# Later loads of one channel tile's up weights, and one tile's deferred convolutions two products later, in a decoder layer with a ConvFFN

## The chip, the cores and the metric

The kernel runs on one core of one Trainium2 chip. The metric is the time of one execution in microseconds (us) on the device. Times of before come from three runs; the profile is of one execution.

## The reference

One decoder layer on 16 meta tokens and 1024 tokens of 1024 features: a mixer (differential attention and a gated recurrence, HGRN2), its output projection, and a feed-forward network with a causal convolution of width 3. The part that matters here is the end of the mixer and the feed-forward network:

```python
mix = jnp.concatenate([y_diff, y_hgrn], axis=-1) @ w_out[l]
h = h + rmsnorm(mix, ln_mix_post[l])
a = rmsnorm(h, ln_ffn_pre[l])
y = conv_ffn(a, w_ffn_up[l], ffn_conv_w[l], ffn_conv_b[l], w_ffn_down[l])
h = h + rmsnorm(y, ln_ffn_post[l])

def conv_ffn(a, w_up, conv_w, conv_b, w_down):
    u = a @ w_up                      # 1024 x 5632
    u = <causal convolution of width 3, one filter per channel>(u) + conv_b
    gate, up = jnp.split(u, 2, axis=-1)
    return (jax.nn.gelu(gate, approximate=True) * up) @ w_down
```

## The kernel before, in words

Every large float32 product is made of three passes: each operand is split into a rounded part ("h") and its rest ("l"), and the matmuls h*h, h*l and l*h are summed. A split is a cast on ScalarE (ACT) and a subtraction on VectorE (DVE) or GpSimd (POOL), issued by the helper `split` at L58's recording wrapper.

Three stages touch the change.

*Output projection and row blocks.* The loop over `i` from 1 to 8 takes a block of 128 tokens. TensorE makes the second half of the projection (`py`); `post(i)` normalizes it on ACT and DVE, adds it to the residual stream in `xh`, stores `xh` to DRAM (`hsc`, L1229), and scales it into `a2`. There are two `xh` buffers, so the load of block i + 2 (L1208) waits for the store of block i. `trans(i - 2)` transposes an earlier block (L1249), and ACT copies it into `at2`.

*Operands of the up products.* `at2` is cut in two token parts, p = 0 and 1. For each part the quarters and their sums and differences become seven split operands `t` (a Strassen-like scheme with seven products). This is a long run of DVE instructions, the `t<-at,t` rows.

*Up products.* Channel tiles are counted by `ft` from 0 to 21. Tile 0 is multiplied plainly (`pq`). From ft = 1 on a tile takes seven products `j` per token part, in the banks `pa`, `pb`, `pc`; DVE combines them (`xu`, `u`, `uu`, `ug`). The seven weight operands of a tile come from four loaded quarters (`ra`, 256 KB each, tags 11, 22, 21, 12; five buffers), POOL sums and differences of them (`ws`), and splits (`uh`, `ul`). `prep(q)` makes operand q % 7 of tile q // 7, and with q % 7 == 0 it issues the four loads. During product j of tile ft the code calls `prep` for tile ft + 1. So the third channel tile (ft = 2) is prepared during ft = 1.

Convolutions are deferred: a finished tile part is put in `later`, and `gated` takes it out during the next tile. `gated` is four DVE instructions for a token part (`c<-ug,cwt,c` and `c<-uu,cwt,c`), a gelu on ACT, a product on POOL and a store to `gsc`.

The order on TensorE is the program's. On the other engines a scheduler sets it at build time; `tc.issue_after(x)` keeps an instruction behind x in the queue of x's engine, with no wait of its own. Each engine and SyncE's DMA queue works in order, so an instruction that waits holds what is behind it.

Of the kernel before, what the change touches and what calls it, by code (L numbers as in the profile page):

```python
# [17 lines left out]
P = 128  # L18
# [72 lines left out]
def layer_kernel(ctx: ExitStack, tc: tile.TileContext, x, meta, table, lbl, gpre, gpost, win,  # L91
# [5 lines left out]
    T, SY = nc.tensor, nc.sync  # L97
# [40 lines left out]
    hsc = dp.tile([SEQ, D], F32, tag="hsc", name="hsc")  # L138
# [30 lines left out]
    def rstd_of(dst, ss, n):  # L169
        A.activation(dst, ss, AF.Ln, bias=eps[: dst.shape[0]], scale=1.0 / n)  # L170
        return A.activation(dst, dst, AF.Exp, scale=-0.5)
# [11 lines left out]
    def long_tile(name):  # L183
        return mix_tile("X0", F32, name)
# [621 lines left out]
    raws, parts = {}, [[None, None] for _ in range(3)]  # L806
# [216 lines left out]
    def tok(i):  # L1023
        return (2, 14) if i == 0 else (P, start(i))
# [46 lines left out]
    blocks, loaded = {}, {}  # L1071
# [60 lines left out]
    at2.reverse()  # L1132
    q_cm, qp = pool("p2", 2, "right")

    raws, sums, made, marks = {}, {}, {}, {}

    def load_raw4(ft):
        raws.clear()
        for nm, m, c in (("11", ft, 0), ("22", ft + NF, 1), ("21", ft + NF, 0), ("12", ft, 1)):
            raws[nm] = swp.tile([P, 512], F32, tag="ra", name=f"ra{ft}_{nm}", bufs=5)  # L1140
            with tc.issue_after(loaded[4].ins):
                SY.dma_start(raws[nm], wup[m][:, 512 * c: 512 * (c + 1)])

    def w_sum(nm, a, b, op):
# [4 lines left out]
    def prep(q):  # L1149
        ft, j = divmod(q, 7)  # L1150
        if ft >= NF or q in made:
            return
        if j == 0:
            load_raw4(ft)
            src = raws["11"]
            w_sum("1", raws["21"], raws["22"], ALU.add)
        elif j == 1:
            src = w_sum("2", sums["1"], raws["11"], ALU.subtract)
        elif j == 2:
            src = sums["1"]  # L1160
        elif j == 3:
            src = w_sum("3", raws["11"], raws["21"], ALU.subtract)
        elif j == 4:
            src = raws["12"]
        elif j == 5:
            src = raws["22"]
        else:
            src = w_sum("4", raws["12"], sums["2"], ALU.subtract)
        where = swp if q % 2 else wp
        hi = where.tile([P, 512], F32R, tag="wh", name=f"uh{q}", bufs=4)  # L1170
        lo = where.tile([P, 512], F32R, tag="wl", name=f"ul{q}", bufs=4)
        split(hi, lo, src, G if j % 2 == 0 and j and (ft > 1 or j != 4) else V, marks.get((ft - 1, 0)) if j == 1 else None)
        made[q] = (hi, lo)
# [3 lines left out]
    def prep_plain():  # L1177
        load_raw4(0)
        for j, nm in enumerate(("11", "12", "21", "22")):
            where = swp if j % 2 else wp  # L1180
            hi = where.tile([P, 512], F32R, tag="wh", name=f"uh{nm}", bufs=4)
            lo = where.tile([P, 512], F32R, tag="wl", name=f"ul{nm}", bufs=4)
            split(hi, lo, raws[nm], G, halved[0])
            plain[nm] = (hi, lo)
# [25 lines left out]
    def post(i, py, free=None):  # L1210
        r, t0 = tok(i)
        xh = xhs.pop(i)
        if i % 2:
            a2 = long_tile(f"a2_{i}")[:, :D]
        elif i == 0:
            a2 = xh
        else:
            a2 = bp.tile([P, D], F32, tag="a2", name=f"a2_{i}", bufs=1)
        tmp = qp.tile([P, 512], F32, tag="tmp", name=f"tmp{i}", bufs=1)
        junk = qp.tile([P, 512], F32, tag="junk", name=f"junk{i}", bufs=1)  # L1220
        s1, s2 = ssy[:r, i, 1:2], ssy[:r, i, 2:3]
        A.activation(junk[:r], py[:r], AF.Square, accum_out=s1)
        V.tensor_tensor(tmp[:r], py[:r], gpo[:r], op=ALU.mult)
        A.activation(s1, s1, AF.Ln, bias=ssy[:r, i, 0:1], scale=1.0 / D)
        A.activation(s1, s1, AF.Exp, scale=-0.5)
        V.scalar_tensor_tensor(xh[:r, :512], y0[:r, i], s1, xh[:r, :512], ALU.mult, ALU.add)
        V.scalar_tensor_tensor(xh[:r, 512:], tmp[:r], s1, xh[:r, 512:], ALU.mult, ALU.add)
        if i:
            SY.dma_start(hsc[P * (i - 1): P * i, :], xh)  # L1229
        if i:  # L1230
            A.activation(a2[:r], xh[:r], AF.Square, accum_out=s2)
        else:
            s3 = ssy[:r, i, 3:4]
            for half, s_ in ((0, s2), (1, s3)):
                A.activation(free[:r], xh[:r, 512 * half:512 * half + 512], AF.Square, accum_out=s_)
            V.tensor_tensor(s2, s2, s3, op=ALU.add)
        marks["scale"] = rstd_of(s2, s2, D)
        marks["normed"] = V.scalar_tensor_tensor(a2[:r], xh[:r], s2, gfb[:r], ALU.mult, ALU.mult)
        a2t[i] = a2
# [61 lines left out]
    for i in range(1, NBLK):  # L1301
# [18 lines left out]
        if i == 1:  # L1320
# [11 lines left out]
            for p in (3, 4):  # L1332
                out_last(p)
            continue
        post(i, py)
        if i == 2:
            post(0, ysum[:, :512], ysum[:, 512:])
# [33 lines left out]
    def gated(ft, p, ug, uu):  # L1371
        cg = conv(ft, p, 0, ug)
        A.activation(cg, cg, AF.Gelu_apprx_tanh)
        cu = conv(ft, p, 1, uu)
        marks["mult"] = G.tensor_tensor(cg, cg, cu, op=ALU.mult)
        marks["store"] = SY.dma_start(gsc[P * ft: P * (ft + 1), C0[p]:C0[p] + 2 * WN[p] - 2], cg)
# [109 lines left out]
    def g_in(k, half, nm):  # L1486
        t = dn.tile([P, 2 * WN[0]], F32, tag="gk", name=f"gi{nm}_{k}")[:, :512]
        SY.dma_start(t, g_src(k, half))
        return t

    def w_in(pr, k):
        t = swp.tile([P, 512], F32, tag="ra", name=f"wi{pr}_{k}", bufs=5)
        if pr in (5, 6, 7, 4):
            SY.dma_start(t, tsc[(5, 6, 7, 4).index(pr)][P * k: P * (k + 1)])
        else:
            kk, half = {1: (k, 0), 2: (k + NH, 0), 3: (k + NH, 1)}[pr]
            SY.dma_start(t, wdown[P * kk: P * (kk + 1), 512 * half: 512 * (half + 1)])
        return t

    def operands(pr, k, loaded=None):  # L1500
        ga, gb, gc, gs = (keep[nm][:, k] if keep else None for nm in ("ga", "gb", "gc", "gs"))
        if pr == 1:
            a = loaded[0] if loaded else g_in(k, 0, "1")
        elif pr == 2:
            SY.dma_start(gb, g_src(k + NH, 0))
            a = gb
        elif pr == 5:
            a = gs
        elif pr == 6:
            V.tensor_tensor(gs, gs, ga, op=ALU.add)  # L1510
            a = gs
        elif pr == 3:
            V.tensor_tensor(gb, gs, gb, op=ALU.subtract)
            a = gb
        elif pr == 7:
            V.tensor_tensor(ga, gc, ga, op=ALU.subtract)
            a = ga
        else:
            a = g_in(k + NH, 1, "4")
        b = loaded[1] if loaded else w_in(pr, k)  # L1520
        nm = f"{pr}_{k}"
        gh = dn.tile([P, 512], F32R, tag="gh", name=f"gh{nm}")
        gl = dn.tile([P, 512], F32R, tag="gl", name=f"gl{nm}")
        split(gh, gl, a, V)
        wh = wp.tile([P, 512], F32R, tag="wh", name=f"wh{nm}", bufs=4)
        wl = wp.tile([P, 512], F32R, tag="wl", name=f"wl{nm}", bufs=4)
        split(wh, wl, b, V)
        return gh, gl, wh, wl

    for ft in range(1, NF):  # L1530
        units = [unit(ft, p, ps_b) for p in range(2)]
        for j in range(7):
            if j != 1:
                with tc.issue_after(marks["gain"].ins) if ft == 1 else nullcontext():
                    prep(7 * (ft + 1) + j)
            for u in units:
                next(u)
            if j in (1, 3):
                with tc.issue_after(marks["last"].ins):
                    gated(*later.pop(0))  # L1540
            if j == 1:
                prep(7 * (ft + 1) + j)
            if ft == NF - 2 and j == 5:
                with tc.issue_after(marks["store"].ins):
                    opens = [(g_in(k, 0, "1"), w_in(1, k)) for k in range(LOOK)]
            if ft == NF - 1 and 1 < j < 5:
                with tc.issue_after(marks["x1"].ins), tc.issue_after(marks[ft, 1].ins):
                    ready[j - 2] = operands(1, j - 2, opens[j - 2])
# [190 lines left out]
```

## Time and profile before

| | us |
|---|---|
| median of three runs (1275.89 to 1278.39) | 1275.97 |
| the profiled execution | 1276.64 |
| its span, first to last instruction | 1274.9 |

Of the span TensorE is busy for 1256.4 us, DVE 914.5, ACT 687.2 and POOL 507.8. The granted clock of TensorE is 0.999. The row blocks lie from about 560 to 620 us, the plain products of tile 0 from 617 to 643 us, and the tiles from ft = 1 on behind them, up to 1045 us.

In the rows of the timeline stand start, duration, engine, line, operation, output<-inputs with the buffer numbers left out, and in brackets how long the engine had been idle and what ended that. In the rows of waits: engine, its tile and line, what it waited for, us in total, times, longest.

### The profile page before, as it was taken

The numbers are of one execution on the slowest core, as the hardware profiler recorded it, in microseconds if no ns is written. First come the engines' busy times: TensorE is split into PE (matmuls) and PEld (weight loads), VectorE is DVE, ScalarE is ACT, GpSimd is POOL, SyncE is SP. The second block draws the span as 40 slices with busy tenths as digits, with TensorE's granted clock in tenths as the row PEclk, the third lists the DMA queues.
The fourth block names the chain that finished last, engine by engine and source line by source line (L and its number), as shares of the span: only waits on it lengthen the run. The fifth ranks groups of instructions, "written<-read, shape, count | busy, mean of one in ns | idle before, by whom it ended". The sixth has DMA issues, their size and how long they took to land.

```text
span 1274.9 us, 26032 instructions
## 1 busy us (share of the span) xinstructions
PE 1256.4 (99%) x10154; PEld 1172.8 (92%) x10154; DVE 914.5 (72%) x1489; ACT 687.2 (54%) x1635; POOL 507.8 (40%) x390
## 2 busy tenths in 40 slices
PE   8999999999999999999999999999999999999997
PEld 7999999999999998778899999999999998888886
DVE  7665646565656564557899888898898877797586
ACT  8475466546654754356764544445535445564554
POOL 5231423241323311353067676676776731020121
PEclk9999999999999999999999999999999999999999
DMA  7335555273734633688322221322222238955363
GB/s 260 96 60 131 89 140 96 80 146 93 132 94 79 125 81 119 217 268 276 129 67 68 92 87 64 100 76 75 92 76 84 75 113 262 355 180 173 91 215 124
DMA packets 116561, 165.04 MB, mean 129 GB/s; under 512 B 10115, under 2 KB 57539, under 8 KB 116438
## 3 DMA queue, kind: packets, MB, share of 16 engines
q1 hardware_dynamic: 93206, 151.84, 37.1%
q0 software_dynamic: 23232, 11.54, 7.7%
q8 instruction: 80, 1.31, 0.4%
q14 instruction: 43, 0.35, 0.1%
HBM read 134.24 MB, written 52.17 MB: 146 GB/s over the span
## 4 chain that ended last, share of the span: by engine, by line
PE 48%; DVE 3%; DMA 1%; ACT 1%; issue 1%; POOL 1%; DVEq 0%; SPq 0%; ACTq 0%; POOLq 0%
PE pd L1586 5%; PE pd L1587 5%; PE pd L1585 5%; PE pb L1412 4%; PE pb L1411 4%; PE pb L1413 4%; PE pa L1412 3%; PE pc L1412 3%; PE pa L1411 3%; PE pc L1411 3%; PE pc L1413 3%; PE pa L1413 3%; PE pq L1390 1%; PE pq L1389 1%; PE pq L1391 1%
## 5 line engine op out<-in xcount | busy, mean ns | idle before, releaser
L1412 PE MATMUL pb<-t,uh 128*128 128x258 f32 x504 | 140.9, 280 | 0.3 <-DVE t L58 0.3
L1411 PE MATMUL pb<-t,uh 128*128 128x258 f32 x504 | 140.5, 279 | 0.8 <-DVE u L58 0.8
L1413 PE MATMUL pb<-t,ul 128*128 128x258 f32 x504 | 140.1, 278 | 0.0
L1586 PE MATMUL pd<-wl,gh 128*128 128x512 f32 x308 | 120.3, 391 | 0.9 <-DVE wl L58 0.9
L1587 PE MATMUL pd<-wh,gl 128*128 128x512 f32 x308 | 120.0, 389 | 0.0
L1585 PE MATMUL pd<-wh,gh 128*128 128x512 f32 x308 | 119.9, 389 | 0.0
L58 DVE SCALAR_TENSOR_TENSOR c<-uu,cwt,c 128x514 f32<-128x514 f32 (+1 forms) x88 | 107.0, 1215 | 0.0
L58 DVE SCALAR_TENSOR_TENSOR c<-ug,cwt,c 128x514 f32<-128x514 f32 (+1 forms) x88 | 101.4, 1153 | 0.0
L1411 PEld LDWEIGHTS pb<-t,uh 128*128 128x128 f32 x504 | 94.8, 188 | 1.0 <-DVE u L58 1.0
L1412 PEld LDWEIGHTS pb<-t,uh 128*128 128x128 f32 x504 | 94.8, 188 | 0.5 <-DVE t L58 0.5
L58 ACT ACTIVATE c<-c 128x514 f32<-128x514 f32 (+1 forms) x44 | 27.9, 634 | 124.7 <-DVE c L58 124.7
L1413 PEld LDWEIGHTS pb<-t,ul 128*128 128x128 f32 x504 | 94.8, 188 | 0.0
L1412 PE MATMUL pa<-t,uh 128*128 128x258 f32 (+1 forms) x336 | 93.9, 280 | 0.0
L1412 PE MATMUL pc<-t,uh 128*128 128x258 f32 (+1 forms) x336 | 93.9, 279 | 0.0
L58 POOL TENSOR_TENSOR ws<-ra,ra 128x512 f32<-128x512 f32 x42 | 69.2, 1648 | 61.8 <-DMA ra<-in_wup_dram 31.4
L1411 PE MATMUL pa<-t,uh 128*128 128x258 f32 (+1 forms) x336 | 93.6, 279 | 0.0
L1411 PE MATMUL pc<-t,uh 128*128 128x258 f32 (+1 forms) x336 | 93.6, 278 | 0.0
L1413 PE MATMUL pa<-t,ul 128*128 128x258 f32 (+1 forms) x336 | 93.4, 278 | 0.0
L1413 PE MATMUL pc<-t,ul 128*128 128x258 f32 (+1 forms) x336 | 93.4, 278 | 0.0
L58 POOL TENSOR_TENSOR ul<-ws,uh 128x512 fp32r<-128x512 f32 x42 | 69.1, 1646 | 60.0 <-PE pa L1413 44.2
L58 POOL TENSOR_TENSOR c<-c,c 128x514 f32<-128x514 f32 (+1 forms) x44 | 67.9, 1543 | 52.6 <-ACT c L58 49.2
L58 DVE TENSOR_TENSOR ul<-ra,uh 128x512 fp32r<-128x512 f32 x43 | 41.5, 966 | 46.6 <-POOL ul L58 46.6
(389 smaller groups left out, 4184.0 us busy)
## 6 DMA issues: line engine op xcount, KB each, us to landing
ra<-in_wup_dram SPq DMA_DIRECT2D x88, 256.0 KB, 2.6
mp<-msc SPq DMA_DIRECT2D x23, 512.0 KB, 5.6
tsc<-in_wdown_dram SPq DMA_DIRECT2D x44, 256.0 KB, 4.8
wi<-tsc SPq DMA_DIRECT2D x44, 256.0 KB, 3.1
gi<-gsc SPq DMA_DIRECT2D x33, 256.0 KB, 4.0
wi<-in_wdown_dram SPq DMA_DIRECT2D x33, 256.0 KB, 5.0
gsc<-c SPq DMA_DIRECT2D x22, 257.0 KB, 2.1
tsc<-in_wdown_dram POOLq DMA_DIRECT2D x22, 256.0 KB, 7.0
```

The costliest lines, as they stand in the source:

```text
L58: ins = call(*args, **kw)
L1389: T.matmul(pt, hi[:, s], th[:, k], start=(kh + k == 0), stop=False)
L1390: T.matmul(pt, hi[:, s], tl[:, k], start=False, stop=False)
L1391: T.matmul(pt, lo[:, s], th[:, k], start=False, stop=(kh == 1 and k == 3))
L1411: T.matmul(pt, hi[:, s], th[:, k], start=(first and k == 0), stop=False, skip_group_check=True)
L1412: T.matmul(pt, hi[:, s], tl[:, k], start=False, stop=False, skip_group_check=True)
L1413: T.matmul(pt, lo[:, s], th[:, k], start=False, stop=(k == 3), skip_group_check=True)
L1585: T.matmul(py, gh[:, s], wh, start=(k == 0 and pr not in (3, 7)), stop=False, skip_group_check=True)
L1586: T.matmul(py, gh[:, s], wl, start=False, stop=False, skip_group_check=True)
L1587: T.matmul(py, gl[:, s], wh, start=False, stop=(k == NH - 1), skip_group_check=True)
```

## The change

The loads of ft = 2 stand behind the store of the seventh row block, `stored[7]`, and no longer behind an early load, `loaded[4]`. The two convolutions that are taken from `later` during ft = 1 (those of tile 0) are issued at the products j = 3 and 5, and no longer at j = 1 and 3. All other tiles stay as they are.

```diff
-    raws, sums, made, marks = {}, {}, {}, {}
+    raws, sums, made, marks, stored = {}, {}, {}, {}, {}
...
-            with tc.issue_after(loaded[4].ins):
+            with tc.issue_after((stored[7] if ft == 2 else loaded[4]).ins):
                 SY.dma_start(raws[nm], wup[m][:, 512 * c: 512 * (c + 1)])
...
-            SY.dma_start(hsc[P * (i - 1): P * i, :], xh)
+            stored[i] = SY.dma_start(hsc[P * (i - 1): P * i, :], xh)
...
-            if j in (1, 3):
+            if j in ((3, 5) if ft == 1 else (1, 3)):
                 with tc.issue_after(marks["last"].ins):
                     gated(*later.pop(0))
```

SyncE's queue at the end of the row blocks. `ra_11_7986`, `ra_22_7988`, `ra_21_7990` and `ra_12_7992` are the four quarters of ft = 2, those of 8249 to 8255 belong to ft = 3; `hsc<-xh_7467` is the seventh store and `hsc<-xh_7521` the eighth.

```order
 L1208 DMA xh_7521<-in_x_dram 128x1024
 L1229 DMA hsc<-xh_7467 128x1024
+L1142 DMA ra_11_7986<-in_wup_dram 128x512
+L1142 DMA ra_22_7988<-in_wup_dram 128x512
+L1142 DMA ra_21_7990<-in_wup_dram 128x512
 L1229 DMA hsc<-xh_7521 128x1024
+L1142 DMA ra_12_7992<-in_wup_dram 128x512
 L1142 DMA ra_11_8249<-in_wup_dram 128x512
 L1142 DMA ra_22_8251<-in_wup_dram 128x512
```

Before, the first of the four left behind the loads of ft = 1, the next two behind the loads of the fourth row block, and the last behind the fourth store. On POOL the order of the three sums that read them (`ws`) is unchanged: they stand behind the last `y<-y,gpo` of the row blocks.

DVE's queue during ft = 1. `c_0_0` is the convolution of tile 0, p = 0; `ul_8079` and `ul_8115` (8068 and 8104 now) are operands 1 and 3 of ft = 2; `u_1_0` and `uu_0` are combinations of ft = 1, p = 0, behind product 3.

```order
 L58 TENSOR_TENSOR xu_0_8003<-pb_0_8037,xu_0_8003 128x258
 L58 TENSOR_TENSOR xu_1_8021<-pb_1_8051,xu_1_8021 128x256
-L58 SCALAR_TENSOR_TENSOR c_0_0_8065<-ug_0_7645,cwt,c_0_0_8065 128x514
-L58 SCALAR_TENSOR_TENSOR c_0_0_8070<-uu_0_7646,cwt,c_0_0_8070 128x514
-L58 SCALAR_TENSOR_TENSOR c_0_0_8065<-ug_0_7645,cwt,c_0_0_8065 128x514
-L58 SCALAR_TENSOR_TENSOR c_0_0_8070<-uu_0_7646,cwt,c_0_0_8070 128x514
-L58 TENSOR_TENSOR ul_8079<-ws_8076,uh_8078 128x512
-L58 TENSOR_TENSOR ul_8115<-ws_8112,uh_8114 128x512
+L58 TENSOR_TENSOR ul_8068<-ws_8065,uh_8067 128x512
+L58 TENSOR_TENSOR ul_8104<-ws_8101,uh_8103 128x512
 L58 TENSOR_TENSOR u_1_0_8004<-pb_0_8037,xu_0_8003 128x258
+L58 TENSOR_TENSOR uu_0_8001<-pc_0_8075,u_1_0_8004 128x258
```

The four instructions of `c_0_0` now stand behind `uu` of both token parts, and those of the second part, `c_0_1`, behind the combinations of product 5. From the first weights of ft = 3 on DVE's queue is as before.

ACT's queue in the same place, now. `uh15_8067` is the cast of operand 1 of ft = 2 and reads the second POOL sum; `t1_5` is the last split of the second token part, and `xu_1_1` the first copy of ft = 1, p = 1.

```order
L58 CAST uh15_8067<-ws2_8065 128x512
L58 CAST t1_5_7960<-at2_1_6973 128x1024
L58 COPY xu_1_1_8021<-pa1_1_8023 128x256
L58 CAST uh16_8071<-ws1_7994 128x512
L58 ACTIVATE c0_0_0_8135<-ug0_0_7645,cbt_85,cwt_84 128x514
L58 ACTIVATE c1_0_0_8140<-uu0_0_7646,cbt_85,cwt_84 128x514
```

The cast of operand 1 stood ahead of the split's cast before, too; what moved is the time at which its POOL sum can have its loads.

## The prediction

> **What bounds the kernel now.** I read the page's engine line first, then the list of what TensorE waited for from 560 us to 700 us, where every moved instruction lies, then the busy time by stretch.
>
> ```profile
> PE 1256.4 (99%) x10154; PEld 1172.8 (92%) x10154; DVE 914.5 (72%) x1489; ACT 687.2 (54%) x1635; POOL 507.8 (40%) x390
> ```
> ```profile
> PE pa L1249 <- DVE a L58: 1.2, 2, 0.7
> PE pb L1411 <- DVE u L58: 0.8, 1, 0.8
> PE pb L1412 <- DVE t L58: 0.3, 1, 0.3
> ```
> ```profile
> 600.00:620.00 20.00, 19.34 (x108) 16.40 (x107) 13.56 (x16) 13.75 (x41) 0.39 (x1) 1.00 0.67 206
> 620.00:640.00 20.00, 19.47 (x166) 19.19 (x165) 19.97 (x19) 17.11 (x31) 0.00 (x0) 1.00 0.19 75
> 640.00:660.00 20.00, 18.86 (x159) 18.46 (x158) 20.00 (x24) 14.94 (x24) 13.98 (x6) 1.00 0.13 40
> 660.00:680.00 20.00, 20.00 (x175) 20.00 (x174) 17.48 (x23) 8.94 (x16) 14.14 (x11) 1.00 0.25 81
> ```
>
> TensorE is the bound, and its matmuls are not changed. Only its waits can go. The stretches' columns are length, PE, weight load, DVE, ACT and POOL busy, clock, DMA share and GB/s. PE is idle for 0.66 + 0.53 + 1.14 = 2.33 us in 600 to 660 us, and not at all from 660 us. At four places it stands still, always for the DVE. A wait costs a little more than its idle time: in the last stretch a matmul starts every 20/175 = 0.114 us, but the one before a wait is counted busy for 0.28 us (rows below), so each of the four costs some 0.17 us more. The ceiling of any gain is therefore 2.33 + 4 x 0.17 = 3.0 us, 0.235% of the time. A measurement of this kernel tells about 0.2%, 2.55 us, from no change. There is no such ceiling on a loss: from 620 to 660 us the DVE is busy 39.97 of 40 us, and what is put on it there comes out on PE.
>
> **What leaves: three sums and four loads from 560 to 604 us.** The third tile's loads feed three POOL sums, which ran here:
>
> ```profile
> 594.73 2.26 POOL L58 TENSOR_TENSOR ws<-ra,ra 128x512 f32<-128x512 f32 x1
> 597.07 1.61 POOL L58 TENSOR_TENSOR ws<-ws,ra 128x512 f32<-128x512 f32 x1
> 598.65 1.74 POOL L58 TENSOR_TENSOR ws<-ra,ra 128x512 f32<-128x512 f32 x1
> 659.25 1.29 POOL L58 TENSOR_TENSOR ws<-ra,ra 128x512 f32<-128x512 f32 x1
> ```
> ```profile
> 596.38 1.16 DVE L58 SCALAR_TENSOR_TENSOR xh<-y,ssy,xh 128x512 f32<-128x512 f32 x1
> 597.46 1.77 DVE L58 SCALAR_TENSOR_TENSOR xh<-tmp,ssy,xh 128x512 f32<-128x512 f32 x1
> 617.25 0.75 DVE L58 SCALAR_TENSOR_TENSOR xh<-tmp,ssy,xh 128x512 f32<-128x512 f32 x1
> ```
>
> The same DVE instruction takes 0.75 us where POOL is idle and 1.77 and 1.16 us beside the sums: they kept it 1.02 and 0.41 us, 1.43 us together. That is on a path to PE:
>
> ```profile
> 599.27 1.06 ACT L58 ACTIVATE a<-xh 128x1024 f32<-128x1024 f32 x1 [3.45 <-DVE xh L58]
> 610.28 0.33 PE L1249 MATMUL pa<-ident,a 128*128 128x128 f32 x1 [0.66 <-DVE a L58]
> 621.12 0.44 PE L1249 MATMUL pa<-ident,a 128*128 128x128 f32 x2 [0.53 <-DVE a L58]
> 619.78 1.28 DVE L58 SCALAR_TENSOR_TENSOR a<-xh,ssy,gfb 128x1024 f32<-128x1024 f32 x1 [1.78 <-ACT ssy L58]
> ```
>
> ACT stood 3.45 us for that xh, with the next block's squares queued behind it; so later blocks' DVE work moves up with it. An advance of 1.43 us covers both waits: PE gains 0.66 + 0.53 + 2 x 0.17 = 1.5 us, and the last "a" and all DVE work behind it start about 1.5 us earlier (the head start). Fewer bytes in the store and load chain of the xh tiles may add to it; between nothing and 1.7 us is possible, and I take 1.5, nearest to the 1.43 of the rows.
>
> **What arrives: the same loads and sums behind the seventh store.** SyncE now issues three loads behind this first store, ahead of the second one, and the fourth behind that:
>
> ```profile
> 618.20 7.43 SPq L1229 DMA_DIRECT2D hsc<-xh  x2
> hsc<-xh SPq DMA_DIRECT2D x6, 512.0 KB, 5.2
> ra<-in_wup_dram SPq DMA_DIRECT2D x6, 256.0 KB, 2.6
> ```
>
> The second store does not leave until 7 us later, so three issues ahead of it cost SyncE nothing. The fourth load waits for the third sum, and the fourth tile's loads stand behind it; those left only from 641 us, so there are 10 us of cover. The loads land after the store ahead of them: between 2.6 us (alone) and 5.2 + 2 x 2.6 us behind 618.2 - 1.5 = 616.7, so from 619 to 627 us; I take 623. The first sum then meets the DVE's longest unbroken run:
>
> ```profile
> 625.20 1.23 DVE L58 TENSOR_TENSOR t<-at,t 128x1032 fp32r<-128x1032 f32 x1
> 629.95 9.28 DVE L58 TENSOR_TENSOR t<-at,t 128x1024 fp32r<-128x1024 f32 x8
> 646.56 1.22 DVE L58 TENSOR_TENSOR t<-at,t 128x1024 fp32r<-128x1024 f32 x1
> 647.84 0.38 PE L1412 MATMUL pb<-t,uh 128*128 128x256 f32 x1 [0.35 <-DVE t L58]
> 631.74 0.28 PE L1390 MATMUL pq<-t,uh 128*128 128x256 f32 x1
> 644.58 6.70 POOL L58 TENSOR_TENSOR ul<-ws,uh 128x512 fp32r<-128x512 f32 x1 [44.18 <-PE pa L1413]
> ```
>
> [...] Bounds: nothing, if sums fall beside DVE work that doesn't mind; 2.26 + 1.61 + 1.74 = 5.6 us, if they hold the DVE for their whole rows. I take three turns, 3.06 us, because mixed DVE work from 622 to 629 us resembles the 597 us place. Less the head start the splits come 3.06 - 1.5 = 1.56 us late. PE waits for the split at 646.56 already, so that is 1.56 us on PE against before. (The split for 631.74, ready by 629.95 + 9.28/8 = 631.11, has 0.63 us of room; it takes part of the delay earlier, not twice.)
>
> [...] The 1.77 us row is less than the two one after the other, 0.75 + 1.29 = 2.04 us, so I keep 1.02.
>
> **The convolutions two blocks later.** Four instructions leave the place ahead of u:
>
> ```profile
> 650.70 1.13 DVE L58 SCALAR_TENSOR_TENSOR c<-ug,cwt,c 128x514 f32<-128x514 f32 x1
> 651.75 1.78 DVE L58 SCALAR_TENSOR_TENSOR c<-uu,cwt,c 128x514 f32<-128x514 f32 x1
> 653.45 1.78 DVE L58 SCALAR_TENSOR_TENSOR c<-ug,cwt,c 128x514 f32<-128x514 f32 x1
> 655.16 1.78 DVE L58 SCALAR_TENSOR_TENSOR c<-uu,cwt,c 128x514 f32<-128x514 f32 x1
> 658.07 0.74 DVE L58 TENSOR_TENSOR u<-pb,xu 128x258 f32<-128x258 f32 x2
> 657.47 0.28 PE L1413 MATMUL pa<-t,ul 128*128 128x256 f32 x1
> 658.53 0.39 PE L1411 MATMUL pb<-t,uh 128*128 128x258 f32 x1 [0.79 <-DVE u L58]
> 652.65 0.60 ACT L58 CAST uh<-ws 128x512 fp32r<-128x512 f32 x1
> ```
>
> They hold 656.86 - 650.70 = 6.2 us. Without them u waits for the cast at 652.65 (0.60), two ul and nothing else: some 654.5 us, 4 us ahead of PE. So the 0.79 + 0.17 = 0.95 us go, even if the splits are 3 us late. The convolutions then run from about 655 us, the second set behind two more combinations; their cover is the DVE's idle 2.5 us of 20 in the last stretch. What could be late next is u of the third tile:
>
> ```profile
> 677.39 0.42 DVE L58 TENSOR_TENSOR u<-pb,xu 128x258 f32<-128x258 f32 x1
> 678.20 0.28 PE L1411 MATMUL pb<-t,uh 128*128 128x258 f32 x1
> ```
>
> It was ready at 677.81, 0.39 us before its matmul. If the convolutions pushed it later by more than that, PE would wait there instead. Its DVE queue is the same as before from the third tile's first weights on, and the two and a half idle microseconds lie ahead of it: cost 0, and what exceeds 0.39 us if that cover is gone.
>
> **The sum.** -1.5 (two waits) is used up where PE catches up with late splits; there PE stands at +1.56, then -0.95: **+0.6 us**. Against the profiled execution's 1276.64 us (span 1274.9 and 1.74 around it) that is 1277.2. The median of the runs shown is 1275.97, 0.67 us less, so on it the forecast is **1276.6 us**; own range 1275.2 (two turns, -0.4, and a little) to 1278.0 (sums of 1.29 us each and a smaller head start).
>
> **Rivals.**
>
> *All waits go (faster).* The loads land while the DVE still does mixed work, the sums fall where it waits for ACT or reads PSUM, and the splits keep their head start. Then PE keeps the 1.5 and gains the 0.95: -2.45 us, at most the ceiling of -3.0; say -2.7, 1273.3 us. For it: the DVE paused 1.78 us for ACT at 619.78. Against it: that pause is before the landing I take, and a DVE busy for 39.97 of 40 us has no free place.
>
> *The sums hold the DVE whole, with no head start (slower).* [...] For it: nothing in the run from 620 to 660 us gives. Against it: ACT's 3.45 us wait names xh's DVE instruction, and 1.77 us is less than two instructions end to end (0.75 + 1.29).
>
> *The sums lose the port (slightly slower).* The 6.70 us row is a POOL instruction of 1.29 us that stood 5.4 us beside back-to-back DVE splits, until these:
>
> ```profile
> 650.03 0.76 DVE L58 TENSOR_TENSOR xu<-pb,xu 128x258 f32<-128x258 f32 x2
> 652.00 0.28 PE L1411 MATMUL pb<-t,uh 128*128 128x258 f32 x1
> ```
>
> So the sums might not run until the DVE itself stops. ACT's order then has the cast of the second sum ahead of the last split's cast and of the second xu copy, and the DVE stops for that cast behind the split at 646.56 and one ul, at 648.4. Two sums (2.6), two casts (0.6 and about 1.0), a split (1.22), an ul and an xu (about 1.1) end at 654.9, where PE wanted xu at 652.00: 2.9 us, less the 0.95: +1.9 us, 1277.9, and with the head start +0.4. It costs less than a delay of every split.
>
> *The edit does nothing.* It could be that the loads would leave no later than before. SyncE's order excludes it: they stand behind the seventh store now.
>
> **How the numbers follow.** The forecast has 0.40, the sums that lose the port 0.08, all waits gone 0.24, the held DVE 0.28. Three of the four put a cost against a gain of the same size, so the signs are nearly even; a loss has no ceiling and a gain has. The range leaves out the edge of the first rival (below 1273.2) and the long end of the second (above 1279.2): 1273.2 to 1279.2. Faster by over 0.2% takes nearly the whole ceiling, a part of 0.24: 0.20. Within 0.2%: 0.40 + 0.08 + 0.04 = 0.52. Slower by over 0.2%: 0.28.
>
> **What would show it.** Right: xh beside no POOL row and 0.75 us both times near 597 us; no PE wait for "a" at 610 and 621 us; no PE wait for u; three ws rows on POOL between 620 and 632 us; splits behind them later, and a PE wait for t longer than 0.35 us by about what the splits are late. Wrong: waits for "a" that stay (no head start); DVE rows of 1.2 us that stay 1.2 us beside the sums (no turns); a ws row of 5 us or more (lost port); or a PE wait for u of the third tile. A time under 1273.0 would mean that something gained outside these four waits.

## The result, and the profile after

The changed kernel takes 1281.67 us (median of 10 runs, 1278.62 to 1284.13), the kernel before 1276.63 (10 runs, 1275.89 to 1278.75). The ratio is 1.0037, with a 95% interval of 1.0028 to 1.0045: slower by about 0.4%, where 1276.6 was forecast and the range ended at 1279.2. The profiled execution took 1280.56 us, 3.92 more than that of before; its span is 1278.8 us against 1274.9.

The list of what TensorE waited for, after:

```profile
PE pq L1390 <- DVE t L58: 2.1, 1, 2.1
PE pb L1412 <- DVE t L58: 1.9, 1, 1.9
PE pb L1411 <- DVE u L58: 1.4, 1, 1.4
```

Both waits for `a` are gone. Two waits for a split `t` of about 2 us stand in their place, where before had one of 0.3 us, and the wait for `u` is another one than before. The timeline of TensorE gives the places:

```profile
631.69 0.42 PE L1390 MATMUL pq<-t,uh 128*128 128x256 f32 x1 [2.15 <-DVE t L58]
650.59 0.38 PE L1412 MATMUL pb<-t,uh 128*128 128x256 f32 x1 [1.91 <-DVE t L58]
681.48 0.39 PE L1411 MATMUL pb<-t,uh 128*128 128x258 f32 x1 [1.42 <-DVE u L58]
```

The same three matmuls started at 631.74, 647.84 and 678.20 us before. So TensorE is level at the first place, 2.75 us late at the second and 3.28 us late at the third. From the third to the end of the span it is 1278.8 - 681.48 = 597.3 us now and 1274.9 - 678.2 = 596.7 before: the loss is complete, but for 0.6 us, at the third tile's `u`.

The DVE and POOL at the first two places, from the timeline:

```profile
595.54 0.74 DVE L58 SCALAR_TENSOR_TENSOR xh<-y,ssy,xh 128x512 f32<-128x512 f32 x1
596.20 0.74 DVE L58 SCALAR_TENSOR_TENSOR xh<-tmp,ssy,xh 128x512 f32<-128x512 f32 x1
617.15 1.28 DVE L58 SCALAR_TENSOR_TENSOR a<-xh,ssy,gfb 128x1024 f32<-128x1024 f32 x1 [1.78 <-ACT ssy L58]
...
623.82 2.21 DVE L58 TENSOR_TENSOR at<-at 128x1032 f32<-128x1032 f32 x1
625.96 2.31 DVE L58 SCALAR_TENSOR_TENSOR a<-xh,ssy,gfb 128x1024 f32<-128x1024 f32 x1
628.20 2.30 DVE L58 TENSOR_TENSOR at<-at 128x1032 f32<-128x1032 f32 x1
...
646.00 2.32 DVE L58 TENSOR_TENSOR at<-at 128x1024 f32<-128x1024 f32 x1
648.24 2.30 DVE L58 TENSOR_TENSOR t<-at,t 128x1024 fp32r<-128x1024 f32 x1
```
```profile
622.41 2.53 POOL L58 TENSOR_TENSOR ws<-ra,ra 128x512 f32<-128x512 f32 x1 [28.47 <-DMA ra<-in_wup_dram]
625.02 2.17 POOL L58 TENSOR_TENSOR ws<-ws,ra 128x512 f32<-128x512 f32 x1
627.16 2.25 POOL L58 TENSOR_TENSOR ws<-ra,ra 128x512 f32<-128x512 f32 x1
645.36 1.88 POOL L58 TENSOR_TENSOR ul<-ws,uh 128x512 fp32r<-128x512 f32 x1 [15.95 <-ACT uh L58]
647.31 2.14 POOL L58 TENSOR_TENSOR ws<-ra,ws 128x512 f32<-128x512 f32 x1
```

The `xh` rows are free of POOL. Three sums cost three DVE instructions 0.98, 1.03 and 1.07 us (they took 1.23, 1.28 and 1.23 before). Then an `ul` and a `ws` cost two more 1.10 and 1.08 us; before, that `ul` had stood for 6.70 us beside DVE rows of 1.22.

ACT and the DVE ahead of the third place:

```profile
669.20 0.63 ACT L58 ACTIVATE c<-c 128x510 f32<-128x510 f32 x1 [3.13 <-DVE c L58]
669.73 0.61 ACT L58 CAST uh<-ra 128x512 fp32r<-128x512 f32 x1
...
671.68 0.35 ACT L58 COPY xu<-pa 128x258 f32<-128x258 f32 x1
```
```profile
669.08 0.74 DVE L58 SCALAR_TENSOR_TENSOR c<-uu,cwt,c 128x510 f32<-128x510 f32 x1
...
672.07 0.43 DVE L58 TENSOR_TENSOR xu<-pb,xu 128x258 f32<-128x258 f32 x1 [0.25 <-ACT xu L58]
673.63 0.69 DVE L58 TENSOR_TENSOR ul<-ws,uh 128x512 fp32r<-128x512 f32 x1 [1.14 <-ACT uh L58]
...
681.01 0.41 DVE L58 TENSOR_TENSOR u<-pb,xu 128x258 f32<-128x258 f32 x1
```

The gelu of the second moved convolution stands 3.13 us at the head of ACT's queue, until the DVE has finished that set. Behind it are casts and the copy of `xu` for the third tile, and for these the DVE waits 0.25 and 1.14 us in turn. `u` comes at 681.01 where it came at 677.39. The same cast, copy and `ul` before:

```profile
668.83 0.61 ACT L58 CAST uh<-ra 128x512 fp32r<-128x512 f32 x1
669.53 1.26 DVE L58 TENSOR_TENSOR ul<-ra,uh 128x512 fp32r<-128x512 f32 x1 [2.45 <-POOL ul L58]
670.06 0.35 ACT L58 COPY xu<-pa 128x258 f32<-128x258 f32 x1
671.05 0.68 DVE L58 TENSOR_TENSOR ul<-ws,uh 128x512 fp32r<-128x512 f32 x1
```

The 2.45 us are the idle time that the prediction took for cover. The row names a POOL `ul`, but that one had ended at 668.87 us. The DVE's `ul` reads the cast beside it, which ended at 669.44, 0.09 us ahead of it: the DVE stood for ACT.

The 3.62 us by which `u` is late arise in three steps. The first `ul` starts 0.90 us late (670.43), since the DVE comes later to this tile. Behind the two waits for ACT the second `ul` is 2.58 us late. The last 1.0 us is one more slow row ahead of `u`, beside POOL: three of 1.77 to 1.79 us, where before had two.

Last, the granted clock, in three stretches of 3.41 us (columns as in the prediction's stretches):

```profile
628.50:631.91 3.41, 1.26 (x10) 1.06 (x10) 3.41 (x3) 3.16 (x6) 0.91 (x1) 1.00 0.20 77
631.91:635.32 3.41, 3.41 (x18) 3.41 (x17) 3.41 (x4) 2.94 (x4) 0.00 (x0) 0.50 0.00 0
635.32:638.73 3.41, 3.41 (x31) 3.41 (x31) 3.41 (x4) 0.37 (x1) 0.00 (x0) 1.00 0.02 5
```

After the first new wait, TensorE ran one stretch at half clock: 18 matmuls where the next has 31. Before had no such stretch between 12 and 1271 us. So there were three suspects: DVE instructions made longer by POOL, the convolutions, and the clock.

### The profile page after: what moved, and what is told of

It is laid out like the page before. It is cut to its first block, busy times and chain, and to the rows that moved or that the text cites. A ratio compares the mean times of both kernels' runs of the same rounds, so it can differ in the third digit from the quotient of the medians.

```text
span 1278.8 us, 26038 instructions
## 1 busy us (share of the span) xinstructions
PE 1257.3 (98%) x10154; PEld 1173.6 (92%) x10154; DVE 916.8 (72%) x1489; ACT 687.5 (54%) x1635; POOL 504.4 (39%) x390
## 4 chain that ended last, share of the span: by engine, by line
PE 44%; DVE 6%; ACT 3%; issue 1%; DMA 0%; DVEq 0%; SPq 0%; ACTq 0%
PE pd L1586 5%; PE pd L1587 5%; PE pd L1585 5%; PE pb L1412 4%; PE pb L1411 4%; PE pb L1413 4%; PE pc L1412 3%; PE pc L1411 3%; PE pc L1413 3%; PE pa L1412 3%; PE pa L1411 3%; PE pa L1413 3%; DVE c L58 1%; DVE xh L58 1%; ACT a L58 1%
## 5 line engine op out<-in xcount | busy, mean ns | idle before, releaser
L1411 PE MATMUL pb<-t,uh 128*128 128x258 f32 x504 | 140.5, 279 | 1.4 <-DVE u L58 1.4
L1413 PE MATMUL pb<-t,ul 128*128 128x258 f32 x504 | 140.2, 278 | 0.0
L1411 PEld LDWEIGHTS pb<-t,uh 128*128 128x128 f32 x504 | 94.8, 188 | 1.6 <-DVE u L58 1.6
L1413 PEld LDWEIGHTS pb<-t,ul 128*128 128x128 f32 x504 | 94.8, 188 | 0.0
L1411 PE MATMUL pc<-t,uh 128*128 128x258 f32 (+1 forms) x336 | 93.6, 278 | 0.0
L1411 PE MATMUL pa<-t,uh 128*128 128x258 f32 (+1 forms) x336 | 93.6, 278 | 0.0
L1413 PE MATMUL pc<-t,ul 128*128 128x258 f32 (+1 forms) x336 | 93.4, 278 | 0.0
L1413 PE MATMUL pa<-t,ul 128*128 128x258 f32 (+1 forms) x336 | 93.4, 278 | 0.0
L58 POOL TENSOR_TENSOR ul<-ws,uh 128x512 fp32r<-128x512 f32 x42 | 64.3, 1531 | 34.5 <-ACT uh L58 34.5
```

The source lines that it names most:

```text
L58: ins = call(*args, **kw)
L1411: T.matmul(pt, hi[:, s], th[:, k], start=(first and k == 0), stop=False, skip_group_check=True)
L1413: T.matmul(pt, lo[:, s], th[:, k], start=False, stop=(k == 3), skip_group_check=True)
```

## The experiments

Ratios are against the kernel before on the same chip, with 95% intervals; a ratio is not the quotient of the two medians and can differ a little from it. One execution of each run is profiled. Where an edit adds lines, the rows of that run have higher line numbers: L1411 of the change is L1413 or L1415 in some. "The port" in the recorded texts is the author's supposition of why DVE rows grow longer beside POOL rows: that they do is measured (by 0.98 to 1.10 us above), a port is in no profile.

**Each part alone.** The loads without the convolutions (the change's first three hunks, the last left out):

> The loads of the third tile behind the seventh store, the convolutions where they were. Only SyncE's queue differs from before. Port theory (POOL's sums and splits take the port from the DVE's unbroken split run): three sums near 622 to 629 us cost the DVE some 1.05 us each, two more POOL instructions near 645 to 649 us another 1.1 us each; PE waits about 2 us for t near 631 and about 2 us near 648 us, the clock is halved for some 3.4 us behind the first wait, and the splits end some 2.8 us later than before. The u behind the convolutions then waits for both, so its 0.8 us wait stays or grows, and no wait for u in the third tile appears. Time 1279 to 1281. Convolution theory (the loss comes from the later convolutions): no more than 1 us from before, 1276 to 1277.6.

Measured: 1279.66 us (12 runs; before 1276.65, 23 runs), ratio 1.0025 (1.0014 to 1.0036). The convolutions without the loads (only this hunk):

```diff
-            if j in (1, 3):
+            if j in ((3, 5) if ft == 1 else (1, 3)):
```

> The convolutions two products later, the loads where they were. Port theory: the waits near 610, 621 and 647 us as before (0.66, 0.53, 0.35), no half clock; the 0.8 us wait for u in the second tile goes, -0.95 us. Convolution theory: ACT stands some 3 us for the last convolution of tile 0 with the third tile's first casts and copies behind it, and PE waits for u of the third tile, 1.4 us and more. If both hold, the time is within 1 us of before, 1275.8 to 1277.3; if the whole loss were the convolutions', 1280 or more.

Measured: 1278.88 us (12 runs), ratio 1.0021 (1.0012 to 1.0031), more than the 1277.3 expected if both held and less than the 1280 of the convolutions alone. The loads alone have the change's two waits for `t`, 2.1 and 1.9 us, and none for `u`. The convolutions alone have this one in the third tile:

```profile
681.96 0.39 PE L1411 MATMUL pb<-t,uh 128*128 128x258 f32 x1 [2.32 <-DVE u L58]
```

Both parts lose by themselves, each by its own waits: the loads by those for `t`, the convolutions by that for `u`. The profiled execution of the convolutions (1280.34 us) is 1.5 us above the median; it also has a half-clock stretch at 520.70 us, ahead of everything that was moved. The move of the convolutions, which the prediction counted as a gain of 0.95 us, costs about as much as that of the loads.

**The sums kept off the splits.** The change, with the three sums held on POOL behind the last `ul` of the second tile:

```diff
+        with tc.issue_after(lows[-1].ins) if late_sums[0] and nm != "4" else nullcontext():
             G.tensor_tensor(sums[nm], a, b, op=op)
```

> The changed kernel with the third tile's three sums held on POOL behind the second tile's last ul (near 645 us). PE's and the DVE's order is that of the changed kernel; ACT has two casts a few places later. Port theory: no DVE instruction of 2.2 us between 620 and 632 us, the split run keeps its head start, no PE wait for t near 631 us and no half clock; POOL's sums come late and are met by the DVE in 645 to 655 us, so a wait near 650 us of 1 to 4 us can remain. Time 1277 to 1280, below the changed kernel. If the loads' lateness itself (and not the port) made the wait near 631 us, that wait stays as it is, about 2.1 us.

Measured: 1283.98 us (6 runs), ratio 1.0059 (1.0045 to 1.0073); 1277 to 1280 was expected.

```profile
628.26 9.29 DVE L58 TENSOR_TENSOR t<-at,t 128x1024 fp32r<-128x1024 f32 x8
674.51 0.39 PE L1415 MATMUL pb<-t,uh 128*128 128x258 f32 x1 [2.92 <-DVE xu L58]
```

With no sum beside them the eight splits begin 1.7 us earlier than before, and the wait near 631 us is gone: the sums made it. The time is not better, because TensorE now waits 2.92 us for `xu` in the third tile. Taking away a wait ahead of the third tile gains nothing while the third tile comes later. The late sums may themselves be what holds the third tile up, and the profile's mean clock is 0.997, as the change's is; this run does not part these. Its profiled execution, 1281.52 us, is the shortest of the six.

**The DVE late, without the change.** The kernel before, with the last gain instruction issued three more times (1.28 us each; by the starts of the rows in its profile 3.84 us):

```diff
+        for _ in range(3 if i == 8 else 0):
+            V.scalar_tensor_tensor(a2[:r], xh[:r], s2, gfb[:r], ALU.mult, ALU.mult)
```

> The kernel before with the eighth row block's last DVE instruction (a, 1.28 us) issued three more times in a row, the same values written again: the DVE is some 3.57 us late from 630 us on, with no load and no POOL instruction moved. Port theory: lateness of the split run is all that counts: PE waits for a and t near 631 us for some 3 us in all, the clock is halved for some 3.4 us as behind the changed kernel's 2.15 us wait, and the time is +3.0 to +4.0 us, 1279.6 to 1280.6; the half clock is hidden behind the splits, which are late anyway. If PE had room in the split run, less than +1.5 us. If the half clock is paid on top, +5 us or more.

Measured: 1286.12 us (6 runs), ratio 1.0060 (1.0040 to 1.0079): four runs at 1285.9 to 1287.1 and two at 1279.9 and 1280.2. The two lie 3.3 and 3.6 us above the kernel before, about what 3.84 us of lateness alone would make. The four, some 6 us longer, have mean clocks of 0.994 and 0.995, the two of 0.997 and 0.998. The profiled one is of the four:

```profile
631.01:634.42 3.41, 0.46 (x4) 0.25 (x3) 3.34 (x4) 0.37 (x1) 0.00 (x0) 1.00 0.00 0
634.42:637.83 3.41, 3.23 (x16) 3.26 (x16) 2.30 (x3) 1.84 (x3) 0.00 (x0) 0.50 0.00 0
```
```profile
649.42 2.32 DVE L58 TENSOR_TENSOR at<-at 128x1024 f32<-128x1024 f32 x1
651.66 2.30 DVE L58 TENSOR_TENSOR t<-at,t 128x1024 fp32r<-128x1024 f32 x1
```

It has half-clock stretches, and also the two long DVE rows near 650 us. So I filled its two waits with 16 matmuls each, which nobody reads:

```diff
+            for _ in range(16 if (i, half) == (8, 0) else 0):
+                T.matmul(pt[:, :256], plain["11"][0][:, :P], tt[0][0][0][:, 0, :256], start=True, stop=True, skip_group_check=True)
...
+        for _ in range(16 if (ft, p) == (1, 1) else 0):
+            T.matmul(pb, made[8][0][:, :P], tt[1][1][0][:, 0], start=True, stop=True, skip_group_check=True)
```

> This is the kernel with three more copies of the last gain instruction (DVE 3.6 us late), and with 16 needless matmuls ahead of each of the two places where TensorE then waits: ahead of the last block's transposes and ahead of the second tile's second product of half 1. [...] 16 x 0.114 = 1.8 us of matmuls fit inside waits of 3.0 us and cost nothing; PE then idles 1.2 to 1.6 us: no halved stretch between 625 and 665 us, all runs at 1279.5 to 1281.5, median 1280.3. Rival (the 6 us are another wait or contention, the clock only goes with them): the median stays at 1285 to 1287, more if the matmuls are not hidden.

Measured: 1281.58 us (8 runs, 1279.86 to 1282.7; before 1277.55, 31 runs), ratio 1.0035 (1.0023 to 1.0046). No run near 1286 is left (up to 1281.5 was expected), and the mean clocks are 0.997 to 0.999, 0.998 in the profile. But the `ul` row there has 7.22 us and the DVE rows beside it 1.23 us, so two things went together, and this pair does not part the clock from the DVE rows.

**The same fill in the changed kernel**, ahead of the product that waits near 631 us, with the changed kernel beside it:

```diff
+                for _ in range(16 if (p, col, side) == (1, 0, 0) else 0):
+                    T.matmul(pt, plain["11"][0][:, :P], tt[1][0][0][:, 0], start=True, stop=True, skip_group_check=True)
```

> The changed kernel with 16 needless matmuls (16 x 0.114 = 1.8 us) ahead of half 1's first plain product, inside the 2.15 us wait for t near 631 us. Half-clock theory: the wait itself stays as late, but TensorE idles only 0.3 us there and its clock is not halved for the next 3.41 us; the copies that ACT makes of its products come earlier, POOL's ul near 645 us finds no turn beside the DVE's splits (as in the seven profiles without a halved stretch near 633 us; in the three with one it did, and it and the sum behind it cost the DVE 2.2 us). The split that TensorE waits for near 649 us is then ready near 648.3 us in place of 650.5, and all behind it is some 2 us earlier: 2 us less than the changed kernel run beside it. Rival (the halved clock is hidden behind the next wait, as its place in the profile suggests): the split is ready at 650.5 as before, the wait for it grows by 1.7 us to 3.6, and the time is that of the changed kernel within 0.7 us.

> The changed kernel once more, beside the others on one chip: 0.3 to 0.5% above the kernel before; a profile of it with a halved stretch near 633 us has the ul near 645 us take about 1.9 us and two DVE instructions of 2.3 us beside it, one without has an ul of about 6.7 us and DVE instructions of 1.22 us.

Measured: 1282.61 us (6 runs), ratio 1.0050 (1.0037 to 1.0063); the changed kernel 1281.67 (5 runs), ratio 1.0045 (1.0032 to 1.0058). No gain. The changed kernel's second profile has the same three waits as the first, 2.1, 1.9 and 1.4 us, and the same mean clock, 0.997. The filled kernel's profile:

```profile
646.29 1.54 POOL L58 TENSOR_TENSOR ul<-ws,uh 128x512 fp32r<-128x512 f32 x1 [16.75 <-ACT uh L58]
646.61 2.30 DVE L58 TENSOR_TENSOR t<-at,t 128x1024 fp32r<-128x1024 f32 x1
681.82 0.39 PE L1413 MATMUL pb<-t,uh 128*128 128x258 f32 x1 [2.31 <-DVE u L58]
```

No stretch at half clock is left there (the clock is 1.00 from 620 to 640 us, where the change has 0.91), and TensorE goes on at 648.97 us behind its wait for `t`, in place of 650.59. All of that is lost again at the third tile's `u`, where it goes on at 681.82, as the change does at 681.48. My claim that the half clock lets POOL's `ul` win its turn is refuted by the first row: here it won without one. So the half clock near 633 us costs the change nothing that these runs show.

**Which convolution.** Loads as before. Only the second one moved, then only the first:

```diff
+            for _ in range(((1, 5) if ft == 1 else (1, 3)).count(j)):
```

> Loads as before; only the second deferred convolution is moved, from product block 3 to 5, and the first stays at 1. Second-set theory: what makes u of the third tile late is the gelu of the second set, which stands at the head of ACT's queue until the DVE has finished that set, ahead of the casts and the copy of xu that the third tile's first products need. Then the wait for u of the second tile stays at 0.8 us, a wait for u of the third tile of 1.5 to 2.5 us appears, and the time is 1.5 to 2.5 us longer: 1278.2 to 1279.2. Rival (the first set's move does it, by filling the DVE later): no wait for u in the third tile, 1276.2 to 1277.2.

```diff
+            for _ in range(((3, 3) if ft == 1 else (1, 3)).count(j)):
```

> Loads as before; only the first deferred convolution is moved, from product block 1 to 3, where it stands just ahead of the second. Second-set theory: the wait for u of the second tile goes (0.95 us), the third tile waits for u by 0.5 us at most: 1275.6 to 1276.3. Rival (the DVE is full, and whatever is put off comes out at the third tile): a wait for u of the third tile of 1.5 to 2.3 us, 1277.5 to 1279.

Measured: second alone 1279.02 us (12 runs; before 1277.55), ratio 1.0017 (1.0007 to 1.0027); first alone 1276.59 (12 runs), ratio 0.9997 (0.9988 to 1.0005). The waits, in this order (the profiled executions are the shortest and the second shortest of their twelve, 1277.02 and 1275.34 us):

```profile
PE pb L1411 <- DVE u L58: 1.9, 2, 1.1
```
```profile
PE pb L1411 <- DVE u L58: 0.5, 1, 0.5
```

With the second one at block 5, `u` is waited for twice, in the second tile (as before) and in the third. With the first one moved, the second tile's wait is gone and 0.5 us is waited in the third. The cost is that of the second convolution's place; the first one's is a small gain at best.

**The change without the second convolution's move.** Loads as in the change, convolutions at 3 and 3:

> The loads as in the change; of the convolutions only the first is moved, to product block 3, and the second stays at 3. If the third tile's u, held back by the second set at block 5, sets the end of the change's loss, then with the second set back the loss is only that of the late splits: waits for t near 631 and 649 us of 2.1 and 1.9 us as in the change, no wait for u in the second tile, 0.7 us at most in the third, 1278.8 to 1279.8, ratio 1.0018 to 1.0026. If the DVE is simply full and lateness adds up wherever the work stands, the third tile still waits for u by 1.4 us or more and the ratio is that of the change, 1.0035 to 1.0045.

Measured: 1280.16 us (7 runs; before 1275.89, 11 runs), ratio 1.0030 (1.0018 to 1.0041). The interval reaches into both expectations and does not part this from the change's 1.0037 or 1.0045. The profiled execution (1278.62 us, the third shortest of seven) shows the waits:

```profile
PE pq L1390 <- DVE t L58: 2.1, 1, 2.1
PE pb L1412 <- DVE t L58: 1.1, 1, 1.1
PE pb L1411 <- DVE u L58: 0.5, 1, 0.5
```

`u` is waited for 0.5 us, and TensorE goes on behind it at 678.97 us, 2.5 us ahead of the change. The wait near 631 us is the same 2.1 us. Behind the second wait for `t` TensorE goes on at 648.97 us, the same time as in the filled kernel. From there on the two kernels differ in the convolutions, and at `u` they lie 2.85 us apart, 678.97 against 681.82. That is the second one's place, in one profile each.

**The loads one block earlier.** Convolutions as before, `stored[6]` in place of `stored[7]`:

> Convolutions as before; the third tile's loads behind the sixth row block's store, one block earlier than in the change. Port theory: each sum costs the DVE 1.0 us only where DVE instructions on SBUF follow each other. The loads leave near 609.8 us and land some 6.6 us later as they did behind the seventh store, so the first sum falls into the DVE's pause of 1.78 us ahead of the last but one gain and two at most cost a turn: wait for t near 631 us 0.6 to 1.3 us in place of 2.1, waits for a 0.3 us or none, time 1277.3 to 1278.7 against 1279.7 with the loads behind the seventh store. Rival (the loads themselves, or a place among later DVE work, set the cost): the wait near 631 us stays at 2 us, 1279.7.

Measured: 1278.09 us (12 runs; before 1277.55), ratio 1.0006 (0.9997 to 1.0015), against 1.0025 behind the seventh store.

```profile
619.61 1.30 POOL L58 TENSOR_TENSOR ws<-ra,ra 128x512 f32<-128x512 f32 x1 [23.64 <-DMA ra<-in_wup_dram]
620.99 2.14 POOL L58 TENSOR_TENSOR ws<-ws,ra 128x512 f32<-128x512 f32 x1
623.08 2.29 POOL L58 TENSOR_TENSOR ws<-ra,ra 128x512 f32<-128x512 f32 x1
```
```profile
620.14 1.85 DVE L58 SCALAR_TENSOR_TENSOR a<-xh,ssy,gfb 128x1024 f32<-128x1024 f32 x1 [1.78 <-ACT ssy L58]
621.91 2.30 DVE L58 TENSOR_TENSOR t<-at,t 128x1032 fp32r<-128x1032 f32 x1
624.74 1.72 DVE L58 TENSOR_TENSOR at<-at 128x1032 f32<-128x1032 f32 x1
```

The first sum begins in a DVE pause and takes 1.30 us, but runs 0.77 us into the next DVE row. The three sums cost the DVE 0.56, 1.08 and 0.49 us (such rows take 1.29, 1.22 and 1.23 where POOL is idle), 2.13 in place of 3.08: the cost goes by what a sum meets. TensorE waits 1.4 us for `t`, but not where the change does. It is at 628.99 us, at a product of the first token part (128x258), and at the second token part there is none. A wait of 1.1 us for `a` is left at 622.05 us, where none or 0.3 us was expected. This profile is of the longest of the twelve runs, 1280.43 us, so its waits do not explain the median.

**A version from this.** The sums early, each in one of the 1.78 us pauses in which the DVE waits for ACT, and only the first convolution moved. Three loads are as before; the fourth stands behind the seventh store. The table `held` has the row block whose `xh` each sum waits for:

```diff
+        made_ = G.tensor_tensor(sums[nm], a, b, op=op)
+        if nm in held:
+            tc.add_manual_dep(made_.ins, folded[held.pop(nm)].ins.name, mybir.DependencyInfo(mybir.DependencyClass.Sync, mybir.DependencyReason.DATA))
...
+            held.update({"1": 4, "2": 6, "3": 7} if ft == 2 else {})
...
+        folded[i] = V.scalar_tensor_tensor(xh[:r, 512:], tmp[:r], s1, xh[:r, 512:], ALU.mult, ALU.add)
```

> Not the change, but what the runs so far point to: three of the third tile's loads as early as before, and the fourth behind the seventh store; each of the three POOL sums waits for one DVE instruction, the last fold into xh of the blocks 4, 6 and 7, so that it runs in the pause of 1.78 us in which the DVE waits for ACT's squares; and the first deferred convolution at product block 3 ahead of the second. Port theory: no DVE instruction between 594 and 625 us is slowed, both waits for a go (1.5 us with the pipeline's refill) and the 0.35 us wait for t with them, the wait for u of the second tile goes (0.95), the third tile waits for u by 0.5 us: 2 us less than before, 0.9982 to 0.9990 of it. Rival (the waits for a are set by ACT's chain, not by the sums): the waits for a stay, 0.9993 to 1.0000 of it, as with the convolution alone.

Measured: 1275.17 us (11 runs, 1273.39 to 1277.52; before 1276.46, 17 runs), ratio 0.9988 (0.9979 to 0.9996).

```profile
597.88 1.30 POOL L58 TENSOR_TENSOR ws<-ra,ra 128x512 f32<-128x512 f32 x1 [3.14 <-DVE xh L58]
610.38 1.29 POOL L58 TENSOR_TENSOR ws<-ws,ra 128x512 f32<-128x512 f32 x1 [11.20 <-issue]
616.46 1.29 POOL L58 TENSOR_TENSOR ws<-ra,ra 128x512 f32<-128x512 f32 x1 [4.79 <-DVE xh L58]
```
```profile
PE pb L1415 <- DVE t L58: 0.8, 1, 0.8
```

Each sum takes 1.3 us and slows no DVE row; both waits for `a` are gone, as expected. In the kernel before, the same sums ran between 594.73 and 600.39 us and cost `xh` 1.43 us; these run no earlier and cost none, so it is the place that counts. By the ratio it is faster than the kernel before by 1.5 us, where 2 were expected: a wait for `t` of 0.8 us is left, the one that was 0.35 us before. With the first convolution's move alone the ratio was 0.9997 (0.9988 to 1.0005), and the two intervals overlap, so what the pauses alone are worth is not shown.

## Why the prediction was wrong

**Right.** The sums had slowed `xh`: without them both rows take 0.74 us and both waits for `a` go. The `a` at 617.15 is 2.63 us earlier than before; 0.85 of that was there at 593 us already, ahead of any moved sum, which leaves 1.78 for the 1.5 taken. The loads left at 615.82 (616.7 assumed) and the first sum began at 622.41 (623). Three turns cost 3.08 us (3.06). The wait for the second tile's `u` went. A turn was counted as 1.02 us, what `xh` had lost beside a sum, and as 1.29 us at the range's upper end. The five rows here lost 0.98 to 1.10; none shows a turn of 1.29 us.

**Mis-sized: the late splits.** The term was +1.56 us, and TensorE stood 2.75 us late at 650 us. Three turns of 3.08 us less the whole 2.63 us by which the DVE came earlier leave 0.45, and the eight splits do start 0.47 us late (630.42 against 629.95). What was missing is two further turns, 2.18 us, by the `ul` at 645.36 and the `ws` behind it. The 6.70 us row had been read for the rival in which the sums stand until the DVE stops, but the rows of 1.22 us beside it also said that the kernel before owes its quick splits to a POOL row that stands. In the profile of the loads with both convolutions at 3, this `ul` lost its turn again (6.72 us), and the wait was 1.1 us in place of 1.9.

**Failed: the step that gave the third tile's `u` no cost.** It said that DVE's queue is unchanged from the third tile's first weights on, and that 2.5 idle microseconds lie ahead. Both are true, and they were not enough. The two sets ran from 658.97 to 669.82 us, not from about 655, and ended 4.7 us later than before. The DVE had been idle because it waited for ACT, and on ACT the second set's gelu now stood ahead of the third tile's casts and copy until the DVE had finished that set. So the DVE waited for ACT again behind it, and one more POOL turn came on top. `u` came 3.62 us late where 0.39 us were free, and "what exceeds 0.39 us" was 3.28 us on TensorE. Of the 2.58 us ahead of that turn, 1.39 are the two waits for ACT; no run moves the gelu alone, so this share is read from the rows, not tested. That the second set's place does it is shown by four runs. The second set alone at block 5 brings the wait, and the first set's move does not. With TensorE 1.6 us earlier ahead of it (the filled kernel), nothing is gained; with the second convolution back, TensorE is 2.5 us earlier behind it.

**The rivals.** "All waits go" did not come. The rival that held the DVE whole comes near the time of the profiled execution (three sums of 1.29 us less the 0.95 give 1278.9, whole rows of 5.6 us 1280.6), but by luck: no row here shows a sum that costs the DVE so much. The rival had no head start and no wait in the third tile; here the head start was real and the loss ended at the third tile's `u`. The sums did not stand until the DVE stopped: each got its turn, with rows of 2.17 to 2.53 us. The half clock was in no case. The two longest runs of the change, 1283.8 and 1284.1 us, have the lowest mean clock, 0.995, and the profiled one has 0.997; so it may be what puts the median 1.1 us above the profiled execution. That is argued, not shown.

## What to carry to other kernels

Before a move is priced at nothing, ask of each in-order queue that it passes what stands behind the moved instructions there, on the engine that feeds the cover as well: an idle stretch that is itself a wait may be no room. Work on an engine that slows another one can be placed where that one waits by design, as the three sums of 1.3 us were here in pauses of 1.78 us, and held there with a dependency. Where several waits lie on one path, price them from the last one backwards, since what is gained ahead of it is given back there.

## What the runs showed of the hardware

In the profile after, full clock is granted for 621.2 us, then half clock for 3.41 us, then full clock again. In the 3.41 us ahead of the half clock TensorE was busy for 1.26 us. A stretch of 3.41 us with 1.63 us, at the same wait of 2.1 us in the changed kernel with both convolutions at 3, was followed by full clock:

```profile
630.66:634.07 3.41, 1.63 (x14) 1.63 (x15) 3.41 (x4) 3.41 (x5) 0.00 (x0) 1.00 0.23 77
634.07:637.48 3.41, 3.41 (x33) 3.41 (x32) 3.41 (x4) 1.80 (x3) 0.00 (x0) 1.00 0.00 0
```

So behind the same wait of 2.1 us the clock was halved in one of these two profiles and not in the other. Why, they do not show.

The `ul` of POOL that becomes ready near 645 us, inside a run of DVE instructions, sometimes gets the next turn and sometimes stands until the run ends. It took 1.54 to 1.89 us in four profiles (the change, the loads alone, the late DVE and the filled change), beside a DVE row of 2.30 or 2.32 us where those rows are shown, and 6.64 to 7.22 us in eight (the kernel before 6.70). It got its turn where it began 0.50 us (the change) and 0.57 us (the late DVE) after the start of a DVE `t` row, and stood where it began 0.29 us after one (the kernel before); behind an `at` row it got it once at 0.82 (the filled change) and stood once at 0.90 (the late DVE with the filled waits). What decides it stays open.
